# Seven block products for both halves of the up projection, and the first half's attention moved to other places

## The chip, the cores and the metric

The kernel runs on one core of one Trainium2 chip. The metric is the device time of one execution in microseconds (us). A time is the median of several runs; the profile is of one further execution, which has its own time.

Five engines work side by side, each with a queue of its own that it takes in order: TensorE (PE: matmuls, with PEld for the weight loads), VectorE (DVE), ScalarE (ACT), GpSimd (POOL), and SyncE (SP), which here issues nearly all transfers. An instruction may wait for others; whatever stands behind it in the same queue then waits too.

## The reference, cut to what matters

```python
SEQ, D_MODEL, D_FF = 2048, 1024, 2816        # 8 gMLP heads, 8 attention heads of 64
h = rms_norm(x, norm_mix_g); z = h @ w_in    # u, v, q, k, v_b, forget logits
out_a = spatial_gating(gelu(u), gelu(v), ...)           # per 128-position block
c = cumsum(log_sigmoid(f_logit))
out_b = softmax(q @ k.T / 8 + c[t] - c[s], s <= t) @ v_b # all 2048 positions, causal
x = x + concat(out_a, out_b) @ w_out
a = causal_conv3(rms_norm(x, norm_ffn_g) @ w_up) + b_conv  # 5632 channels
g, val = split(a)
x = x + (silu(g) * val) @ w_down
out = rms_norm(x, norm_final_g)
```

All inputs are float32. The kernel keeps float32's precision by splitting each operand of a large product into a high and a low part and computing three products (high·high, high·low, low·high).

## The kernel before

**Halves and blocks.** The 2048 positions are two halves of 1024, each of two blocks of 512, so there are four blocks tb = 0 to 3. `mm3` emits the three matmuls for each 128-deep slice of a product; a matmul of 128x512 is the unit of the work.

**Phase A** (`phase_a`, `a_half`) computes for each half keys and queries, values, and the gated heads; keys, queries, values and gated outputs go to DRAM tensors (`kx`, `qx`, `vd`, `mixh`, `mixl`). The first half goes in the order keys and queries, values, gated; the second half gated, values, keys and queries.

**Attention** is a Python generator, `b_stream`, over 32 pieces (8 heads for each tb). A piece has two parts, `b_max` and `b_mix`, and each yields 4·(tb+1) steps:
- a step of `b_max` has two matmuls into a PSUM tile `s`, a minimum over it on DVE (tile `part`) and an exponential with a sum on ACT (`s<-s,part`);
- a step of `b_mix` has two matmuls into `s`, an exponential on ACT (`e<-s`), a copy of its high part on ACT (`ph<-e`), the low part on DVE (`pl<-e,ph`), and two matmuls into `o`.

`s` has three buffers, `e` three, `ph` and `pl` two. Keys and values are read for 512 positions at a time (tiles `m` and `v`, two buffers each).

**What sets the order.** `mm3` calls `tick` after each matmul. `tick` adds 1 to a credit and runs one step of the stream when the credit reaches the rate:

```python
        if self.fill is not None:
            self.credit += 1
            while self.fill is not None and self.credit >= self.rate:
                self.credit -= self.rate
                self.step()
```

`need(tb)` emits steps until block tb is done. The code's order is not the final one: a scheduler that plans with a model of its own writes each engine's queue, and a step's instructions are given a priority 100 places ahead (`AHEAD_B`). So emitted steps may stand later in the queue than the code has them.

**After phase A.** `c_half(0)` multiplies the mixed heads of the first half with `w_out` and normalizes the rows. `d_half(0)` then does the first half's FFN: for each pair of channel groups (22 groups f of 128 gate and 128 value channels) `d_up` computes the up projection (24 matmuls for each of gate and value in each block, so 96 for a group), the convolution and the gate, and `d_down` multiplies the result at once with `w_down` (48 matmuls for a group), adding into `acc`. The attention stream runs on inside `c_half(0)` and `d_half(0)`, and its last pieces are taken by `need(3)` near `d_half`'s end.

**The second half.** `c_late` is `c_half` for the second half. `late_half` then computes the up projection by seven block products for each group f (`up_mms`, `prod`: P1 to P7, 12 matmuls each, so 84 instead of 96), from sums of weight blocks made by `up_sums` and sums of activations made once. `up_conv` does the convolution and the gate, and GpSimd's queue stores the result (`act_d[f]`). `down_half(1)` reads these back and multiplies with `w_down`, with eight PSUM banks `D`.

**Weights.** `load_unit` reads 512 KB into `raw` (two buffers), casts the high part on GpSimd (`whi<-raw`) and makes the low part on DVE (`wlo<-raw,whi`).

Of the kernel before, what the change touches and what calls it, by code (L numbers as in the profile page):

```python
# [31 lines left out]
RATES = [3.5, 4.0, 5.0, 4.6]  # L32
# [18 lines left out]
def f32(ap):  # L51
    return ap.bitcast(F32)


class Block:
# [44 lines left out]
    def need(self, tb):  # L100

        while self.done < 8 * (tb + 1):
            self.step()
# [76 lines left out]
    def constants(self):  # L180
# [19 lines left out]
        self.rows_d = t("rows", 8, [P, D])  # L200
# [36 lines left out]
    def phase_a(self):  # L237
        tc = self.tc
        with ExitStack() as es:
# [15 lines left out]
            def consts():  # L255
                with tc.issue_after(after):
                    self.a_consts(sp, pp)
                    self.b_consts()
# [4 lines left out]
            self.need(0)  # L263
            self.flush()

# [102 lines left out]
    def a_half(self, half):  # L368
# [28 lines left out]
        def keys_queries():  # L397
# [7 lines left out]
            groups = (("k", (2, 3)), ("q", (0, 1)), ("q", (2, 3))) if half == 0 else (("k", (2, 3)), ("q", (0, 1, 2, 3)))  # L405
            for kind, cs in groups:
                with self.tc.issue_after(self.rows_ins), self.tc.issue_after(self.pow_ins):
                    us = [(c, self.a_unit(kind, c)) for c in cs]
                for b in range(2):
                    for c, u in us:  # L410
                        channels(kind, c, *u, b)
                    if half == 1 and kind == "q" and b == 0:
                        self.need(0)
                        self.mix0 = self.load_mix(0)
# [16 lines left out]
        def gated():  # L431
# [5 lines left out]
            for t, ps in token_major(0):  # L437
                if t % 2 == 0:
                    self.a_mixed(vns[t // 2])
                self.a_gate(half * 2 + t // 4, t % 4, ps, vns[t // 2][:, t % 2, :])  # L440
                if half == 0 and t % 4 == 3:
# [131 lines left out]
    def b_consts(self):  # L573
        nc, bp = self.nc, self.bp
        ones = self.til(self.sp, [P, TB], F32, "st")[:2, :]
        nc.gpsimd.memset(ones, 1.0)
        for i in range(2):
            self.dma(self.ones_d[:, i * TB:(i + 1) * TB], ones)
        for k in self.kx:
            self.dma(k[:, 128:130, :], self.ones_d.unsqueeze(0).broadcast_to([8, 2, HALF]))  # L580
        self.mask = bp.tile([P, TB], BF16, name="mask")
# [5 lines left out]
        self.maskT = bp.tile([P, P], BF16, name="maskT")  # L587
# [4 lines left out]
        self.rowsel = bp.tile([8, 4, P], BF16, name="rowsel")  # L592
# [4 lines left out]
        self.M1 = [bp.tile([P, TB], F32R, name=f"m1_{j}") for j in range(2)]  # L597
        self.T1 = [bp.tile([P, TB], F32R, name=f"t1_{i}") for i in range(2)]
# [166 lines left out]
    def c_half(self, half, accp):  # L765
        nc, pp = self.nc, self.dpp
        w_out = self.a["w_out"][0].rearrange("(c p) n -> p c n", p=P)
        acc = []
        mix = [self.mix0, None]
        for b in range(2):  # L770
            mh, ml = mix[b]
            rows = []
            for t in range(4 * b, 4 * b + 4):
                x = self.til(accp, [P, D], F32, "acc")
                t0 = half * HALF + t * P
                self.dma(x, self.a["x"][0, t0:t0 + P, :])
                acc.append(x)
            for col in (b, 1 - b):
                if b == 0 and col == 1:
                    self.need(2 * half + 1)  # L780
                    mix[1] = self.load_mix(2 * half + 1)
                cs = slice(col * 512, (col + 1) * 512)
                if b == 0 or col == 0:
                    us = [self.load_unit(w_out[:, 2 * j:2 * j + 2, cs], 512) for j in range(4)]
                    wh = [us[k // 2][0][:, k % 2, :] for k in range(KC)]
                    wl = [us[k // 2][1][:, k % 2, :] for k in range(KC)]
                for t in range(4):
                    ts = slice(t * P, (t + 1) * P)
                    ps = self.til(pp, [P, TB], F32, "mm")
                    self.mm3(ps, [mh[:, k, ts] for k in range(KC)], [ml[:, k, ts] for k in range(KC)], wh, wl)  # L790
                    ac = acc[b * 4 + t]
                    nc.vector.tensor_tensor(ac[:, cs], ps, ac[:, cs], op=ALU.add)
                    if col == 1 - b:
                        row = self.til(self.dp, [P, D], F32, "ar")
                        r = self.row_scale(self.dp, ac, row)
                        nc.gpsimd.tensor_scalar(row, ac, r, 0.0, ALU.mult, ALU.add)
                        rows.append(row)
            hi, lo = self.hT[b] = self.parts(b)

            def turn(c, rows=rows, hi=hi, lo=lo):  # L800
                self.transpose_split(pp, "dn", [r[:, c * P:(c + 1) * P] for r in rows],
# [456 lines left out]
```

## Time and profile before

| what | value |
|---|---|
| median of 3 runs | 2564.45 us (2561.37 to 2567.49) |
| the profiled execution: its time, its span | 2568.74 us, 2567.0 us |
| PE busy | 2503.3 us, 98% of the span |
| VectorE busy | 1705.5 us, 66% |
| ScalarE busy | 1271.4 us, 50% |
| GpSimd busy | 302.6 us, 12% |
| granted TensorE clock, mean | 0.992 |
| transfers | 336.27 MB, 131 GB/s over the span |

The stages can be told by their tiles in the trace: phase A to about 640 us, `c_half(0)` and `d_half(0)` from there to 1776 us, `c_late` to about 1877 us, the seven products from 1878.5 to 2313 us, and `down_half(1)` from 2318.0 us to the end. Rows of groups give "busy us, mean ns of one | idle us of the engine before them, and what ended it". Rows of windows give the busy us of each engine in that stretch, the number of its instructions, the granted clock, the share of the transfer engines and GB/s.

### The profile page before, as it was taken

The page shows a single profiled execution, that of the slowest core. Times are in us where ns is not written, and L with a number is a line of the kernel's source. Part 1 is how long each engine was busy: PE and PEld are TensorE (multiplying, and loading weights), DVE is VectorE, ACT ScalarE, POOL GpSimd, SP SyncE. Part 2 cuts the span into 40 slices and gives each one's busy share as a digit, 9 for nine tenths or more (in the row PEclk, how much of TensorE's full clock was granted, in tenths as well). Part 3 has the DMA queues.
Part 4 walks back from the last instruction along what each step waited for, and adds up shares of the span by engine and source line. Part 5 has one row for each costly group of instructions (what it writes and reads, how often), then busy time and mean ns, then how long its engine had stood idle before and what let it go on. Part 6 is the DMA issues. An engine that isn't in the chain of part 4 may idle for free.

```text
span 2567.0 us, 32644 instructions
## 1 busy us (share of the span) xinstructions
PE 2503.3 (98%) x11346; PEld 2048.8 (80%) x11346; DVE 1705.5 (66%) x2997; ACT 1271.4 (50%) x2392; POOL 302.6 (12%) x336
## 2 busy tenths in 40 slices
PE   8999999999999999999999999999989999999998
PEld 6787777878788888888888888887868888887887
DVE  5237666555467777777777776766478888875443
ACT  4327777554356555455545544554245454544331
POOL 3204121000111011001100100111200000000000
PEclk9999999999999999999999999999999999999999
DMA  6863534666733333324323332347412222226461
GB/s 186 251 161 101 168 99 133 174 185 206 276 118 115 98 106 106 98 81 119 98 91 98 111 96 81 118 142 250 149 57 82 91 82 82 83 95 231 142 224 55
DMA packets 316032, 336.27 MB, mean 131 GB/s; under 512 B 49724, under 2 KB 218884, under 8 KB 315852
## 3 DMA queue, kind: packets, MB, share of 16 engines
q1 hardware_dynamic: 312700, 322.65, 41.6%
q0 software_dynamic: 3168, 11.54, 1.1%
q8 instruction: 90, 1.47, 0.2%
q14 instruction: 74, 0.61, 0.1%
HBM read 267.80 MB, written 66.46 MB: 130 GB/s over the span
## 4 chain that ended last, share of the span: by engine, by line
PE 86%; DMA 4%; DVE 4%; ACT 3%; issue 1%; POOL 1%; SPq 0%; POOLq 0%; DVEq 0%; ACTq 0%
PE mm L172 12%; PE mm L174 12%; PE mm L176 12%; PE D L1164 9%; PE dn L172 3%; PE dn L176 3%; PE dn L174 3%; PE A L1033 3%; PE A L1032 3%; PE A L1034 3%; PE s L656 2%; PE s L655 2%; PE s L717 2%; PE s L716 2%; PE o L705 2%; PE o L704 2%
## 5 line engine op out<-in xcount | busy, mean ns | idle before, releaser
L172 PE MATMUL mm<-thi,whi 128*128 128x512 f32 x960 | 376.9, 393 | 2.6 <-DVE vn L381 2.6
L174 PE MATMUL mm<-tlo,whi 128*128 128x512 f32 x960 | 377.3, 393 | 0.0
L176 PE MATMUL mm<-thi,wlo 128*128 128x512 f32 x960 | 376.9, 393 | 0.2 <-DVE wlo L126 0.2
L664 ACT ACTIVATE s<-s,part 128x512 f32<-128x512 f32 (+3 forms) x320 | 190.7, 596 | 214.7 <-DVE part L659 139.1
L728 DVE TENSOR_TENSOR pl<-e,ph 128x512 fp32r<-128x512 f32 (+1 forms) x320 | 203.5, 640 | 110.7 <-PE o L705 66.7
L172 PE MATMUL mm<-whi,thi 128*128 128x512 f32 x640 | 254.5, 400 | 8.0 <-POOL whi L114 6.3
L174 PE MATMUL mm<-wlo,thi 128*128 128x512 f32 x640 | 255.1, 399 | 3.1 <-DVE wlo L126 3.0
L176 PE MATMUL mm<-whi,tlo 128*128 128x512 f32 x640 | 253.1, 396 | 0.0
L722 ACT ACTIVATE e<-s 128x512 f32<-128x512 f32 (+1 forms) x320 | 166.9, 533 | 169.8 <-PE s L717 83.5
L727 ACT ACTIVATE ph<-e 128x512 fp32r<-128x512 f32 (+1 forms) x320 | 179.5, 568 | 132.3 <-PE o L704 118.6
L114 POOL TENSOR_SCALAR whi<-raw 128x1024 fp32r<-128x1024 f32 x130 | 148.2, 1142 | 801.7 <-PE mm L176 229.4
L172 PEld LDWEIGHTS mm<-thi,whi 128*128 128x128 f32 x960 | 180.8, 188 | 41.1 <-DVE vn L381 3.1
L174 PEld LDWEIGHTS mm<-tlo,whi 128*128 128x128 f32 x960 | 180.8, 188 | 37.9
L176 PEld LDWEIGHTS mm<-thi,wlo 128*128 128x128 f32 x960 | 180.9, 188 | 37.9 <-DVE wlo L126 0.7
L126 DVE TENSOR_TENSOR wlo<-raw,whi 128x1024 fp32r<-128x1024 f32 x130 | 163.1, 1257 | 59.4 <-POOL whi L114 59.2
L659 DVE TENSOR_REDUCE part<-s 128x1 f32<-128x512 f32 x192 | 128.0, 684 | 44.6 <-PE s L656 43.5
L850 DVE TENSOR_TENSOR acc<-dn,acc 128x512 f32<-128x512 f32 x176 | 120.9, 687 | 52.4 <-PE dn L176 51.2
L172 PEld LDWEIGHTS mm<-whi,thi 128*128 128x128 f32 x640 | 121.5, 190 | 33.9 <-POOL whi L114 7.8
L174 PEld LDWEIGHTS mm<-wlo,thi 128*128 128x128 f32 x640 | 121.8, 190 | 29.7 <-DVE wlo L126 6.6
L1164 PE MATMUL D<-dh,ah 128*128 128x512 f32 x352 | 138.3, 393 | 5.2 <-ACT ah L913 5.2
L176 PEld LDWEIGHTS mm<-whi,tlo 128*128 128x128 f32 x640 | 121.5, 190 | 24.1
L172 PE MATMUL dn<-whi,ar 128*128 128x512 f32 x352 | 138.2, 393 | 0.0
(299 smaller groups left out, 5525.6 us busy)
## 6 DMA issues: line engine op xcount, KB each, us to landing
m<-kx SPq DMA_DIRECT2D x160, 256.0 KB
raw<-in_w_up_dram SPq DMA_DIRECT2D x44, 512.0 KB
rawl<-in_w_up_dram SPq DMA_DIRECT2D x44, 512.0 KB
rawl<-in_w_down_dram SPq DMA_DIRECT2D x44, 512.0 KB
m<-kx SPq DMA_DIRECT2D x160, 136.0 KB
raw<-in_w_in_dram SPq DMA_DIRECT2D x40, 512.0 KB
v<-vd SPq DMA_DIRECT2D x80, 256.0 KB
x<-in_x_dram SPq DMA_DIRECT2D x24, 512.0 KB
```

The lines of the kernel that those rows point to most:

```text
L114: self.cast_ins = self.nc.gpsimd.tensor_scalar(out, in_, 1.0, 0.0, ALU.mult, ALU.add).ins
L126: nc.vector.tensor_tensor(lo, raw, f32(hi), op=ALU.subtract)
L172: mm(ps, lhsT=ah[k], rhs=bh[k], start=k == 0, stop=False)
L174: mm(ps, lhsT=ah[k], rhs=bl[k], start=False, stop=False)
L176: mm(ps, lhsT=al[k], rhs=bh[k], start=False, stop=k == n - 1)
L659: nc.vector.tensor_reduce(dst, ps, axis=AX.X, op=ALU.min)
L664: nc.scalar.activation(ps[:, :n], ps[:, :n], AF.Exp, scale=-1.0, bias=dst, accum_out=ls[:, tt, sb:sb + 1])
L722: nc.scalar.activation(e[:, c], ps[:, c], AF.Exp, scale=-1.0)
L727: nc.scalar.activation(ph[:, c], e[:, c], AF.Copy)
L728: nc.vector.tensor_tensor(pl[:, c], e[:, c], f32(ph[:, c]), op=ALU.subtract)
L850: nc.vector.tensor_tensor(ac, ps, ac, op=ALU.add)
L1164: nc.tensor.matmul(bank[t, col], lhsT=x[i][:, ts], rhs=w[j][:, cs], start=f == 0 and i + j == 0, stop=f == NF - 1 and i == 1)
```

## The change

The first half now takes the second half's path. `c_late` becomes `c_half(half)`, `late_half` becomes `up_half(half)`, and `d_up`, `d_down`, `d_half` and `d_out` go. The order of stages (`run`) is: phase A, `c_half(0)`, `up_half(0)`, `down_first`, `c_half(1)`, `up_half(1)`, `down_half(1)`.

- The first half's up projection has 22·84 matmuls instead of 22·96.
- Both halves of phase A go keys and queries, values, gated. Attention is cut in two lists: the first 20 pieces (tb 0, tb 1 and four heads of tb 2) run in phase A, which ends with `drain()`; the other 12 run in `down_first`, which ends with `drain()` too. `up_half(0)` has no attention.
- `up_conv` stores the first half's results in `act_d`, and the new `down_first` reads them and `w_down` back, 256-row units of 512 columns at a time, in each of two blocks (so `w_down` is read twice), with four PSUM banks `D0`. The rows before the FFN go through `rows_d`.
- The attention pools are closed after phase A and opened again before `down_first`, in the space that `up_half`'s activations and convolution tiles had.

```diff
-RATES = [3.5, 4.0, 5.0, 4.6]
+RATES = [3.7, 3.7, 2.6]
+EARLY = 4
...
+        keys_queries()
+        values()
         if half == 0:
-            keys_queries()
-            values()
-            self.start_fill(self.b_stream([(h, tb) for tb in range(4) for h in range(8)]), RATES[0])
-            gated()
+            pieces = [(h, tb) for tb in range(4) for h in range(8)]
+            self.pieces = pieces[:16 + EARLY], pieces[16 + EARLY:]
+            self.start_fill(self.b_stream(self.pieces[0]), RATES[0])
         else:
-            self.rate = RATES[1]
-            gated()
-            values()
-            keys_queries()
+            self.ready = True
+        gated()
+        self.rate = RATES[1]
...
+    def down_first(self):
...
+            def prep(n):
+                b, col, j = n // (NF), n // (NF // 2) % 2, n % (NF // 2)
+                cs = slice(col * 512, (col + 1) * 512)
+                w = self.load_unit(w_down[:, 2 * j:2 * j + 2, cs], 512)
+                xf = self.til(dp, [P, 2, TB], F32, "df2")
+                for i in range(2):
+                    self.dma(xf[:, i, :], self.act_d[2 * j + i][:, b * TB:(b + 1) * TB])
+                x = [self.til(dp, [P, 2, TB], F32R, "ah2"), self.til(dp, [P, 2, TB], F32R, "al2")]
+                self.both(x, xf)
+                parts.append((w, x))
+
+            prep(0)
+            self.bp_steps(6)
...
+                        for t in range(4):
+                            ts = slice(t * P, (t + 1) * P)
+                            for c in range(2):
+                                for i, k in ((0, 0), (0, 1), (1, 0)):
+                                    nc.tensor.matmul(banks[t], lhsT=x[i][:, c, ts], rhs=w[k][:, c, :],
+                                                     start=j + c + i + k == 0, stop=j == NF // 2 - 1 and c + i == 2)
+                                    self.tick()
...
+                    if (b, col) == (1, 0):
+                        self.need(2)
+                        self.mix0 = self.load_mix(2)
+            self.drain()
+            self.mix1 = self.load_mix(3)
...
+        self.phase_a()
+        for half in range(2):
+            self.accp = cstack.enter_context(tc.tile_pool(name="accp", bufs=1, reuse_waits="tile"))
+            if half:
+                self.down_first()
+            self.dpp = cstack.enter_context(tc.tile_pool(name="dps", bufs=1, space=PSUM, reuse_waits="tile"))
+            self.bstack.close()
+            self.open_half()
+            self.c_half(half)
+            cstack.close()
+            self.up_half(half)
+            self.ustack.close()
+            self.tqs.close()
+            if half == 0:
+                for i in range(2):
+                    self.up_conv(NF - 2 + i)
+                self.ystack.close()
+                cstack = self.c_open()
+                self.b_open()
+                self.b_consts()
+                self.start_fill(self.b_stream(self.pieces[1]), RATES[2])
+        self.down_half(1)
```

Counted over the whole built program, PE has 11019 instructions instead of 11283, DVE 2832 instead of 2998, ACT 2164 instead of 1965, GpSimd 299 instead of 338 and SP 1258 instead of 1130.

**The order on PE, last pieces of attention.** In the program before, the pieces of tb 3 stand among the matmuls of `d_half`. In these rows `mm` is the up projection, `dn` the down projection, `s` and `o` attention:

```order
L174 MATMUL dn_15580<-wlo_15528,ar_15445 128x512
L176 MATMUL dn_15580<-whi_15527,ar_15445 128x512
L172 MATMUL mm_15641<-thi_6872,whi_15603 128x512
L174 MATMUL mm_15641<-tlo_6873,whi_15603 128x512
L176 MATMUL mm_15641<-thi_6872,wlo_15604 128x512
L655 MATMUL s_13149<-m_1_491,t_1_493 128x512
L656 MATMUL s_13149<-m_3019_13117,t_3015_13110 128x512
L172 MATMUL mm_15641<-thi_6872,whi_15603 128x512
L655 MATMUL s_13161<-m_0_490,t_1_493 128x512
L705 MATMUL o_12780<-pl_13077,v_13016 128x128
```

In the changed program most pieces of tb 3 stand behind the matmuls of `down_first` and behind the first 216 matmuls of `c_half(1)`, with only their own kind around them:

```order
L714 MATMUL o_15153<-ph_15206,v_15157 128x512
L726 MATMUL s_15290<-t_1_2433_11425,m_1_2433_11423 128x512
L727 MATMUL s_15290<-t_3279_14494,m_3496_15285 128x512
L715 MATMUL o_15153<-pl_15207,v_15157 128x512
L714 MATMUL o_15153<-ph_15225,v_15216 128x512
L715 MATMUL o_15153<-pl_15226,v_15216 128x512
L714 MATMUL o_15153<-ph_15238,v_15216 128x512
L726 MATMUL s_15304<-t_1_2433_11425,m_1_2433_11423 128x512
L727 MATMUL s_15304<-t_3279_14494,m_3496_15285 128x512
L715 MATMUL o_15153<-pl_15239,v_15216 128x512
```

This stretch is rows 7040 to 7656 of PE's 10743: 595 matmuls of attention (541 when each is counted by its width of 512), 12 matmuls of `c_half(1)` and 22 small transposes and turns. It holds 80 steps of `b_max` and 110 of `b_mix`. In the program before, the longest run of attention matmuls without other work is 9 rows.

**The order on PE, end of phase A.** The last pieces before `c_half(0)` goes on. Here, too, the changed program has attention alone (rows 3120 to 3297, 174 matmuls, 151.5 by width, 15 steps of `b_max` and 36 of `b_mix`), where the program before goes on in the same place with phase A's own products:

```order
L172 MATMUL mm_6393<-whi_6180,thi_6022 128x512
L174 MATMUL mm_6393<-wlo_6181,thi_6022 128x512
L176 MATMUL mm_6393<-whi_6180,tlo_6023 128x512
L172 MATMUL mm_6393<-whi_6186,thi_6022 128x512
L716 MATMUL s_6365<-t_0_492,m_0_490 128x512
L716 MATMUL s_6379<-t_0_492,m_0_490 128x512
```

```order
L665 MATMUL s_6825<-m_0_79_498,t_0_79_500 128x512
L666 MATMUL s_6825<-m_1537_6785,t_1511_6660 128x512
L726 MATMUL s_6851<-t_1_79_501,m_1_79_499 128x512
L727 MATMUL s_6851<-t_1391_6199,m_1550_6846 128x512
L726 MATMUL s_6864<-t_1_79_501,m_1_79_499 128x512
L727 MATMUL s_6864<-t_1391_6199,m_1550_6846 128x512
```

The cover has moved: `c_half(0)`'s first block and part of its second now stand ahead of these rows.

**The order on SP, from `up_half(0)` to `down_first`.** In the changed program the first act rows that `down_first` reads (tile `df`, `df2` in the code) stand behind the loads of the reopened attention tiles:

```order
L74 DMA v_11741<-vd_78 128x4x128
L74 DMA v_11799<-vd_78 128x4x128
L74 DMA t_0_2433_11424<-ones_d 2x512
L74 DMA t_1_2433_11425<-ones_d 2x512
L74 DMA df_2437_11450<-act_104 128x512
L74 DMA df_2437_11450<-act_105 128x512
```

The tiles `t` lie where the convolution's tiles were, so these loads can go only when GpSimd's stores of the last `act_d` rows have landed. The program before had no such place: `d_half(0)` came straight behind `c_half(0)`, and `act_d` was read back only once, in `down_half(1)`.

More of the change, by code (lines that the diff above doesn't have):

```diff
@@ L102, in need, with drain @@
         while self.done < 8 * (tb + 1):
+            self.step()
+            self.count += 3
+            while self.late and self.late[0][0] <= self.count:
+                self.late.pop(0)[2]()
+    def drain(self):
+        while self.fill is not None:
             self.step()
@@ L199, in constants @@
         self.mixl = t("mixl", 4, [D, TB])
-        self.rows_d = t("rows", 8, [P, D])
+        self.rows_d = t("rows", 16, [P, D])
         self.act_d = t("act", NF, [P, HALF])
@@ L763, in load_mix @@
         return hi, lo
[L765 to L801, printed above, removed]
-                                     self.g_ffn[:, c:c + 1], hi[:, c, :], lo[:, c, :])
-            for c in range(KC):
-                self.defer(26 + 8 * c, lambda c=c, turn=turn: turn(c))
-        self.acc = acc
@@ L1131, in down_half, with bp_steps @@
+    def bp_steps(self, n):
+        for i in range(n):
+            self.step()
     def down_half(self, half):
```

212 lines of the change are left out of this document (77 added, 135 removed), and 2 rows, old and new, of the table BUFS.

## The prediction

> **What bounds the kernel now.** I read the busy totals first, then windows through the stages, then the waits of PE.
>
> ```profile
> PE 2503.3 (98%) x11346; PEld 2048.8 (80%) x11346; DVE 1705.5 (66%) x2997; ACT 1271.4 (50%) x2392; POOL 302.6 (12%) x336
> ```
>
> PE is idle for 64 us of 2567.0. The windows (busy us of PE, PEld, DVE, ACT, POOL; granted clock; share of the transfer engines; GB/s) show that this holds with attention in the mix and without:
>
> ```profile
> 340.00:420.00 80.00, 74.05 (x360) 59.23 (x358) 62.37 (x133) 60.42 (x108) 28.45 (x19) 1.00 0.34 102
> 560.00:640.00 80.00, 80.00 (x372) 65.89 (x371) 44.78 (x96) 38.79 (x89) 5.27 (x5) 1.00 0.68 201
> 640.00:720.00 80.00, 78.41 (x347) 64.06 (x346) 38.40 (x70) 27.88 (x66) 14.47 (x15) 0.98 0.75 256
> 1000.00:1200.00 200.00, 200.00 (x903) 165.31 (x902) 151.57 (x292) 103.91 (x221) 22.61 (x24) 1.00 0.35 103
> 1730.00:1780.00 50.00, 48.58 (x221) 39.76 (x219) 40.00 (x67) 28.36 (x53) 7.78 (x11) 1.00 0.81 254
> 1877.00:1900.00 23.00, 14.80 (x63) 10.38 (x61) 22.37 (x27) 11.49 (x13) 0.93 (x1) 0.91 0.25 69
> 2000.00:2100.00 100.00, 100.00 (x438) 81.84 (x437) 84.13 (x105) 52.19 (x80) 2.66 (x5) 1.00 0.25 81
> ```
>
> From 1000 to 1200 us (`d_half` with attention) PE never stops, and ACT is at 52%: attention's ACT work is hidden under matmuls of the FFN. From 2000 to 2100 us (seven products, no attention) PE never stops either, with DVE at 84%. So the time is PE's count of matmuls, as long as other PE work stands around attention. One place differs: from 1877 to 1900 us, where the second half goes from `c_late` to the products, PE is idle for 8.2 us.
>
> The rate of PE comes from the down projection, 1056 matmuls of one shape (first and last start):
>
> ```profile
> L1164 PE MATMUL D<-dh,ah x352: 389/389/794, 2318.0 to 2558.9; 128*128 128x512 f32 x176
> L1164 PE MATMUL D<-dh,al x352: 388/389/389, 2323.8 to 2559.3; 128*128 128x512 f32 x176
> ```
>
> (2559.3 - 2318.0)/1056 = 0.2285 us for each; the window at 2000 gives 0.2283.
>
> **What the change removes.** 22·12 = 264 matmuls of 128x512, all on the path: 264 · 0.2285 = **-60.3 us**. What ACT gains (199 instructions) and DVE exchanges in `up_half(0)` costs nothing: the window at 2000 us shows the same work at full PE. That cover has no attention in it, and neither has the new stage.
>
> **What it adds: attention without cover.** The two orders of PE are the point. Before, no more than 9 attention matmuls stand together. In the changed program 595 do before the second half of `c_half(1)`, and 174 at the end of phase A. There the time is that of the slowest engine of attention itself. Its instructions (mean ns of one behind the comma):
>
> ```profile
> L664 ACT ACTIVATE s<-s,part 128x512 f32<-128x512 f32 (+3 forms) x320 | 190.7, 596 | 214.7 <-DVE part L659 139.1 <-DVE part L661 60.7 <-DVE halo L823 5.3
> L664 ACT ACTIVATION_READ_ACCUMULATOR s<-s,part 128x1 f32 x320 | 63.0, 197 | 0.1
> L722 ACT ACTIVATE e<-s 128x512 f32<-128x512 f32 (+1 forms) x320 | 166.9, 533 | 169.8 <-PE s L717 83.5 <-DVE s L720 52.2 <-DVE pl L728 27.2
> L727 ACT ACTIVATE ph<-e 128x512 fp32r<-128x512 f32 (+1 forms) x320 | 179.5, 568 | 132.3 <-PE o L704 118.6 <-DVE pl L728 4.6 <-issue 3.1
> L739 ACT ACTIVATE op<-o 64x512 f32<-64x512 f32 x32 | 19.0, 594 | 32.1 <-PE o L705 31.7
> L659 DVE TENSOR_REDUCE part<-s 128x1 f32<-128x512 f32 x192 | 128.0, 684 | 44.6 <-PE s L656 43.5
> L728 DVE TENSOR_TENSOR pl<-e,ph 128x512 fp32r<-128x512 f32 (+1 forms) x320 | 203.5, 640 | 110.7 <-PE o L705 66.7 <-ACT ph L727 38.2 <-ACT a L820 2.4
> ```
>
> A step of `b_max` costs ACT 596 + 197 = 793 ns, DVE 684 and PE two matmuls (457); a step of `b_mix` costs ACT 533 + 568 = 1101 ns, DVE 640 and PE four (914). ACT is the slowest in both.
>
> Late stretch: 80 · 0.793 + 110 · 1.101 = 184.6 us, and the ends of seven pieces (`op` and, for each pair of heads, two more of about the same length, some 1.2 us a piece) 8.5: 193.1 us of ACT. PE has 541 matmuls by width, 541 · 0.2285 = 123.6 us, and that part was paid before too. So at least 69.5 us are new. The upper bound is ACT at the highest share that a window shows, 60.42/80 = 0.755: 193.1/0.755 = 256, 132 new. In that window PE was the bound, so the truth lies near the lower end: I take ACT's sum and 10% for waits between engines and for the loads of keys, 212.4, thus **+88.8 us**.
>
> End of phase A: 15 · 0.793 + 36 · 1.101 + 3 = 54.5 us of ACT against 151.5 · 0.2285 = 34.6 of PE: 19.9 at least, 72.2 - 34.6 = 37.6 at most; with 10%, **+25.4 us**.
>
> The other 4 pieces and the first of tb 3 stand among the 1056 `D0` matmuls and the 216 of `c_half(1)`, and their ACT work is hidden as now.
>
> **The seams.** From `up_half(0)` to `down_first`, PE's last product must first pass through the tail of the convolution, then the store, then SP's loads, since the reopened tiles lie where the convolution's were. The groups of that tail, in its order, with the split of a 512 KB tile on ACT (`dh<-rawl`) as the last:
>
> ```profile
> L1097 ACT ACTIVATE cv<-A 128x512 f32<-128x512 f32 x22 | 12.8, 581 | 0.4 <-PE A L1034 0.4
> L1120 ACT ACTIVATE ts<-cv,colB 128x1024 f32<-128x1024 f32 x44 | 54.7, 1244 | 28.4 <-DVE cv L1095 27.8
> L1121 DVE SCALAR_TENSOR_TENSOR ts<-cv,colA,ts 128x1024 f32<-128x1024 f32 x44 | 56.5, 1284 | 22.0 <-ACT ts L1120 21.8
> L1122 DVE SCALAR_TENSOR_TENSOR ts<-cv,colA,ts 128x1024 f32<-128x1024 f32 x44 | 56.4, 1282 | 0.8
> L1126 ACT ACTIVATE cv<-ts 128x1024 f32<-128x1024 f32 x22 | 23.4, 1061 | 6.9 <-DVE ts L1122 6.7
> L1127 DVE SCALAR_TENSOR_TENSOR ts<-cv,ts 128x1024 f32<-128x1024 f32 x22 | 26.8, 1218 | 1.2 <-ACT cv L1126 1.2
> L1128 DVE TENSOR_TENSOR ts<-ts 128x1024 f32<-128x1024 f32 x22 | 26.8, 1219 | 0.1
> L913 ACT ACTIVATE dh<-rawl 128x1024 fp32r<-128x1024 f32 x44 | 45.9, 1048 | 7.8 <-DMA rawl<-in_w_down_dram 6.0 <-PE D L1164 1.7
> ```
>
> The stores of `act` (issue in ns, then us to landing), and two loads of attention's tiles as they stand in the chain that ended last (start, us):
>
> ```profile
> L1129 POOL DMA_DIRECT2D act<-ts x22: 531/533/767, 1933.9 to 2331.6; - x22
> DMA to landing us min/median/max: 2.9/2.9/5.5
> ```
>
> ```profile
> 304.17 3.66 DMA m<-kx
> 315.85 4.60 DMA t<-qx
> ```
>
> The tail is 7.9 us, issue and landing of the store 3.4, a load 3.7 to 4.6 (256 KB, as `m` and `t`), GpSimd's clearing of the tiles some 0.5, and the split of the first rows 1.05: about 17 us. Behind such a gap PE starts slowly:
>
> ```profile
> 1779.86 0.40 PE L176 MATMUL mm<-whi,tlo 128*128 128x512 f32 x1
> 1784.44 1.22 PE L172 MATMUL mm<-whi,thi 128*128 128x512 f32 x2 [4.19 <-POOL whi L114]
> 1787.15 0.63 PE L174 MATMUL mm<-wlo,thi 128*128 128x512 f32 x1
> 1787.57 0.63 PE L176 MATMUL mm<-whi,tlo 128*128 128x512 f32 x1
> 1793.02 0.39 PE L174 MATMUL mm<-wlo,thi 128*128 128x512 f32 x1
> 1793.24 0.39 PE L176 MATMUL mm<-whi,tlo 128*128 128x512 f32 x1
> ```
>
> After 4.19 us of idling matmuls stand 0.42 us apart instead of 0.23, for some 5.6 us: 3 us lost. The seam is **+20 us**; 8 (the tail alone) to 27.
>
> From `c_half(0)` to `up_half(0)` the first half now has the seam that the second has at 1877 us: 8.2 us idle and 2 for the clock, **+10** (0, if fewer things are late, to 14).
>
> Behind the late stretch, the second block of `c_half(1)` needs the last heads: four end operations on ACT and DVE (some 3.3 us), store 2.9, load 4.2, clock 3: +14. In its place the 4.19 us wait and its slow clock (7) go, since `w_out` can be loaded during the stretch: **+7** (0 to 14).
>
> **Transfers in `down_first`.** Its rows on SP, from its first weight load to its last, move 81.8 MB (23.6 of `w_down`, 23.1 of act rows, the rest attention's and the rows'), while PE's 1056 + 254 matmuls take 299 us: 274 GB/s. Nothing before asks for that for so long; the windows at 640 and 1730 us show 256 and 254 GB/s with PE at 98 and 97%. At 256 it takes 320 us, +21; with no stall 0; at the 201 GB/s of 560 us, where PE did not ask for more, +108. I take **+10**, halfway between no stall and 256 GB/s.
>
> **Sum.** -60.3 + 88.8 + 25.4 + 20 + 10 + 7 + 10 = +100.9 us. Against the profiled execution that is 2568.74 + 100.9 = 2669.6; the median is 4.3 us below that execution, so 2564.45 + 100.9 = **2665 us**.
>
> **Rivals.**
>
> 1. *The clock falls in the uncovered stretches.* PE is busy there for only some 58%. If the granted clock halved (0.427 us for each matmul, as between 1784 and 1790 us), PE would be the bound: 541 · 0.427 = 231 us and 151.5 · 0.427 = 65, new 107 + 30 instead of 114: 2688 us. Against it: the window at 340 us has PE idle for 6 us in pieces with the clock at 1.00. The Trainium skill, "TensorE: Matmul & The Clock Gate", section "A second HAM failure mode: psum-queue depth-cycling", says that frequent short idling between groups of matmuls makes the clock gate swing between half and full rate; by it this rival would be the forecast, but the rows so far show the loss only behind a gap of 4 us. Chance 0.08.
> 2. *`down_first` starves.* SP's queue is in order, `raw` and `df2` have two buffers each, and weight loads stand among loads that wait for attention's buffers. Then it runs at the 201 GB/s above, +108 instead of +10: 2763 us. For it: 274 GB/s is asked. Against: PE is at 97% at 254 GB/s. Chance 0.10.
> 3. *ACT does not bound the stretches,* since `b_max` of one piece overlaps `b_mix` of another and the engines run at PE's pace. Then 114 us go: 2551 us, faster. With my other terms it decides when the two stretches lose under 13 us; ACT's instructions alone make it 89. Chance 0.05.
>
> **How the numbers follow.** The forecast has 0.74, the rivals 0.08, 0.10 and 0.05; 0.03 is left for a part of the third that ends near no change. The lower ends of the terms give -60.3 + 69.5 + 19.9 + 8 = +37, 2602 us. The upper ends of the stretches and seams give -60.3 + 132 + 37.6 + 27 + 14 + 14 + 10 = +174, 2739 us. The range 2602 to 2740 holds the forecast and rival 1 and leaves out 2 and 3. About 0.2% (5 us) can be told from no change: faster 0.05, same 0.03, slower 0.92.
>
> **What the new profile would show.** ACT at over 85% and PE near 60% in one stretch of about 210 us, ahead of the last 150 `mm` matmuls of `c_half(1)`, and in one of about 60 us after phase A; PE's waits there on `s`, `ph` and `pl`. An idle PE of some 17 us before the first `D0`. `up_half(0)` with PE full, in some 430 us. The forecast is wrong if ACT in the late stretch stays under 150 us, if PE waits on DMA or `wlo` for tens of us among the `D0` matmuls, or if the clock there is well below 1.

## The result: 2713 us, slower by 5.8%

| | median | runs |
|---|---|---|
| before | 2565.95 us | 2561.37 to 2567.49, 4 runs |
| changed | 2713.12 us | 2708.90 to 2717.81, 4 runs |

The ratio is 1.0577, 95% interval 1.0552 to 1.0602: +147 us, where +101 was forecast (2665, range 2602 to 2740). The spans of the two profiled executions differ by 141.8 us (2708.8 against 2567.0); the readings below are made against that.

The page of the changed kernel, totals and the granted clock in 40 slices:

```profile
PE 2528.3 (93%) x11082; PEld 2012.9 (74%) x11082; DVE 1780.3 (66%) x2831; ACT 1400.2 (52%) x2593; POOL 263.1 (10%) x297
PEclk9999999999989999999699999987999999999999
```

PE has 264 instructions fewer and is busy 25 us longer, and idle for 180 us instead of 64. So part of the loss is idle time and part is matmuls that run slowly; the clock's row shows three dips. Windows of the changed kernel at these places, with the same columns as before (busy us of PE, PEld, DVE, ACT, POOL; granted clock; transfer share; GB/s):

```profile
750.00:818.00 68.00, 51.38 (x188) 33.06 (x187) 42.14 (x98) 54.14 (x123) 2.21 (x4) 0.85 0.38 118
818.00:880.00 62.00, 57.27 (x268) 45.76 (x267) 41.84 (x57) 24.70 (x31) 9.33 (x8) 0.97 0.41 136
880.00:1300.00 420.00, 413.36 (x1788) 337.20 (x1788) 352.48 (x427) 215.32 (x342) 12.69 (x23) 0.99 0.24 77
1300.00:1346.00 46.00, 2.98 (x8) 1.83 (x7) 13.50 (x12) 4.05 (x5) 9.51 (x17) 0.53 0.95 333
1346.00:1670.00 324.00, 321.77 (x1425) 263.50 (x1425) 217.54 (x337) 163.32 (x332) 49.81 (x48) 0.99 0.66 214
1740.00:1960.00 220.00, 188.40 (x639) 120.57 (x638) 143.23 (x293) 172.41 (x401) 0.00 (x0) 0.85 0.45 137
```

They are: the end of phase A (attention alone up to 809.8 us, then a wait), the end of `c_half(0)`, `up_half(0)`, the seam, `down_first`, and the late stretch of attention alone. `up_half(0)` and `down_first` run with PE full, as forecast; the two attention stretches and the seam carry the loss. Four waits of PE, from the end of phase A, the seam and the late stretch:

```profile
PE dn L157 <- ACT acc L833: 8.0, 1, 8.0
PE s L665 <- DMA t<-ones_d: 43.0, 1, 43.0
PE mm L182 <- DMA thi<-mixh: 8.9, 1, 8.9
PE s L665 <- ACT s L674: 9.3, 14, 1.5
```

The first is `c_half(0)`'s: its rows were stored by 738 us, but their normalization stands behind attention in ACT's queue and starts at 812.4.

### The profile page after: what moved, and what is told of

It reads as the page before. It is cut to its first block, busy times and chain, and to the rows that moved or that the text cites. A ratio compares the mean times of both kernels' runs of the same rounds, so it can differ in the third digit from the quotient of the medians.

```text
span 2708.8 us, 32673 instructions
## 1 busy us (share of the span) xinstructions
PE 2528.3 (93%) x11082; PEld 2012.9 (74%) x11082; DVE 1780.3 (66%) x2831; ACT 1400.2 (52%) x2593; POOL 263.1 (10%) x297
## 4 chain that ended last, share of the span: by engine, by line
PE 74%; DMA 6%; DVE 4%; ACT 4%; issue 2%; POOL 0%; SPq 0%; DVEq 0%; POOLq 0%; ACTq 0%
PE D L1054 9%; PE D L1111 9%; PE A L910 6%; PE A L911 6%; PE A L912 6%; PE mm L182 5%; PE mm L186 5%; PE mm L184 4%; PE B L911 3%; PE B L912 3%; PE B L910 3%; PE s L665 2%; PE s L726 2%; PE s L666 2%; DMA m<-kx 2%; PE s L727 2%
## 5 line engine op out<-in xcount | busy, mean ns | idle before, releaser
L124 POOL TENSOR_SCALAR whi<-raw 128x1024 fp32r<-128x1024 f32 x108 | 130.0, 1205 | 750.0 <-PE D L1054 215.4
L665 PE MATMUL s<-m,t 96*128 96x512 f32 (+2 forms) x320 | 132.5, 434 | 70.6 <-DMA t<-ones_d 43.0
L796 DVE TENSOR_TENSOR al<-df,ah 128x1024 fp32r<-128x1024 f32 (+1 forms) x88 | 87.4, 996 | 124.4 <-ACT ah L795 123.5
L795 ACT ACTIVATE ah<-df 128x1024 fp32r<-128x1024 f32 (+1 forms) x88 | 74.1, 845 | 181.1 <-PE D L1111 101.4
L136 DVE TENSOR_TENSOR wlo<-raw,whi 128x1024 fp32r<-128x1024 f32 x108 | 133.3, 1234 | 44.0 <-POOL whi L124 43.7
L665 PEld LDWEIGHTS s<-m,t 96*128 96x128 f32 x320 | 65.8, 210 | 110.2 <-ACT s L674 45.2
L1000 DVE SCALAR_TENSOR_TENSOR ts<-cv,colA,ts 128x1024 f32<-128x1024 f32 x88 | 113.8, 1293 | 48.4 <-ACT ts L999 47.7
L726 PE MATMUL s<-t,m 128*128 128x512 f32 (+1 forms) x320 | 126.7, 397 | 15.1 <-ACT s L674 8.0
L1054 PE MATMUL D<-whi,ah 128*128 128x512 f32 x352 | 139.7, 397 | 0.3 <-ACT ah L795 0.3
L1054 PE MATMUL D<-wlo,ah 128*128 128x512 f32 x352 | 138.8, 394 | 0.0
```

The costliest lines, as they stand in the source:

```text
L665: nc.tensor.matmul(ps[:, :n], lhsT=t1[0:96, ts], rhs=m1[0:96, :n], start=True, stop=False)
L726: nc.tensor.matmul(ps[:, c], lhsT=m1[:, ks], rhs=t1[:, c], start=True, stop=False)
L1054: nc.tensor.matmul(banks[t], lhsT=x[i][:, c, ts], rhs=w[k][:, c, :], start=j + c + i + k == 0, stop=j == NF // 2 - 1 and c + i == 2)
```

## The experiments

Each time stands beside runs of the kernel before on the same chip (medians 2568 to 2569); ratios are to those.

### Is it attention at all? (e5, e6)

Both kernels were run without attention. In the diff for the changed kernel (the same for the kernel before), the stream emits no piece, and attention's rows of `mixh`/`mixl` are zeroed once:

```diff
+        for m in self.mixh + self.mixl:
+            for r in range(512, 1024, P):
+                self.dma(m[r:r + P, :], tf)
...
         for h, tb in pieces:
+            self.done += 1
+            yield
+        return
```

> The kernel before without its attention: no piece is computed, and the attention rows of mixh/mixl are zeros. Attention is 377 us of PE at full clock (95 + 282 in the windows), so if it costs there only its matmuls, the time is about 2190 us (2170 to 2220).

> The changed kernel without its attention, in the same way. T1 (nearly all of the loss is attention that stands without enough other work): what stays of the change is -60 us of matmuls and the two seams, some 30 to 45 and 5 to 18 us, so this kernel is within -30 to +10 us of e5's, where with attention the difference is +147. Rival (the new stage and its transfers cost it, attention or not): 60 us or more above e5's.

Measured: 2148.72 us (2145.38 to 2150.26) for e5, 2151.44 us (2149.91 to 2152.30) for e6: +2.7 us. (e5 is 21 us below the range expected: attention holds PE busy for 416 us in the kernel before, 2503.3 less 2087.7 without it, not for 377.) The new stage and the seven products together cost nothing net: PE is busy 50.7 us less in e6's profile than in e5's and idle 56.0 more, since the seam is there without attention too. The wait in e6:

```profile
PE D L1063 <- ACT ah L804: 45.9, 3, 43.9
```

So 144 of the 147 us are there only when attention is.

### The seam (e1, e8)

In the changed kernel SP's in-order queue issues this while PE idles (start, issue us):

```profile
1297.43 4.82 SPq L74 DMA_DIRECT2D acc<-rows  x6
...
1312.62 2.63 SPq L74 DMA_DIRECT2D tlo<-mixl  x1
...
1326.61 4.37 SPq L74 DMA_DIRECT2D m<-kx  x4
...
1338.49 2.40 SPq L74 DMA_DIRECT2D t<-ones_d  x2
1341.12 0.82 SPq L74 DMA_DIRECT2D df<-act  x2
```

The last store of `act` had been issued at 1311.82. The rows of `acc` and the mixed heads, which nobody needs yet, stand ahead of what PE waits for. e1 holds them behind the first `df` loads:

```diff
-                                self.dma(rows[t], self.rows_d[4 * b + t])
+                                with tc.issue_after(self.dfi):
+                                    self.dma(rows[t], self.rows_d[4 * b + t])
...
-            self.mix1 = self.load_mix(3)
+            with tc.issue_after(self.dfi):
+                self.mix1 = self.load_mix(3)
```

> Changed kernel, but on SP's queue the reads of rows into acc and of the last two blocks of mixh/mixl stand behind the first reads of act rows (df), instead of ahead of them. T1 (SP's in-order queue makes the seam): PE's idle time between up_half(0) and the first attention matmul falls from 43.0 us to the 17 of the tail's chain (15 to 24), and the time by 20 to 27 us against the changed kernel, to about 2690. Rival (the tail of the convolution and the reopened tiles make the seam, or the transfers as such, wherever they stand): idle stays at 35 or more, the time within 8 us of 2713.

Measured: 2718.49 us (ratio 1.0581, 1.0557 to 1.0605), no faster. The idle time fell only from 43.0 to 33.8 us, since a second chain lay right behind the first one. Its links in e1 (GpSimd and SP, start and us):

```profile
1314.02 0.58 POOL L1008 DMA_DIRECT2D act<-ts  x1 [3.64 <-DVE ts L1007]
1318.13 0.52 POOL L592 MEMSET mask<- 128x512 bf16 x1 [3.53 <-DMA act<-ts]
...
1322.81 0.98 POOL L611 MEMSET m<- 8x512 f32 x2
...
1327.73 1.97 SPq L74 DMA_DIRECT2D t<-ones_d  x2
1329.89 0.82 SPq L74 DMA_DIRECT2D df<-act  x2
```

The last product starts at 1299.19, so the tail up to the store takes 14.8 us, not the 7.9 of the forecast. Then the store lands, GpSimd clears the reopened tiles for some 6 us, the rows of ones are loaded, and then the act rows. The 9 us gained were lost in the late stretch, 234 us there instead of 220 (it begins with 12 more rows of attention in PE's order). e8 shortens that second chain:

```diff
-            nc.gpsimd.memset(f32(m[64:128, :]), 0.0)
-            nc.gpsimd.memset(f32(m[96:104, :]), 1.0)
+            nc.vector.memset(f32(m[64:128, :]), 0.0)
+            nc.vector.memset(f32(m[96:104, :]), 1.0)
         for t in self.T1:
-            nc.gpsimd.memset(f32(t[64:128, :]), 0.0)
-            self.dma(f32(t[66:68, :]), self.ones_d[:, 0:TB])
+            nc.vector.memset(f32(t[64:128, :]), 1.0)
```

> e1_seam, with the constants of the reopened attention tiles written by VectorE instead of GpSimd, and the rows of ones in t written in the same memset instead of by two transfers. If the seam is a chain (tail 14 us, store 4, memsets 6, ones 4, act rows 4), PE's idle time there goes from 33.8 to 22 to 27 us and the time 7 to 12 us below e1's. If the act rows would come no sooner, it stays at 31 or more.

Measured: 2711.43 us (1.0565, 1.0542 to 1.0588). The median is 7 us below e1's, but the runs overlap. The wait is 28.9 us, above the 22 to 27 expected, and hangs on another load, `t<-cc`, that stands behind six loads of `raw`. A chain cut at one link hung on the next. What removes most of it is e10, below: other work for PE in the meantime.

### What bounds attention that stands alone (e2, e3)

e2 takes a copy of the late pieces away from ACT:

```diff
-            nc.scalar.activation(ph[:, c], e[:, c], AF.Copy)
+            if self.second:
+                nc.gpsimd.tensor_scalar(ph[:, c], e[:, c], 1.0, 0.0, ALU.mult, ALU.add)
+            else:
+                nc.scalar.activation(ph[:, c], e[:, c], AF.Copy)
```

> Changed kernel, but for the 12 late pieces the copy ph<-e is made on GpSimd instead of ACT; the order on PE is nearly the same. T1 (ACT's instructions bound the uncovered stretch): ACT's work in it falls from 172 us to about 112, VectorE's 143 is then the largest, and the stretch falls from 220 us to 165 to 190, the time by 30 to 55 us. T2 (the stretch is bound by waits within one piece, by the chain s to e to ph to pl to o, which a slower copy on GpSimd lengthens): the stretch stays at 210 to 240 and the time within 15 us of 2713. T3 (the halved clock makes PE the bound): the stretch stays near 220 with the clock still near 0.85.

Measured: 2718.64 us (1.0588, 1.0573 to 1.0604). The window of the stretch, from the last product ahead of it (1741.9) to PE's last `o` (1966.6):

```profile
1742.00:1967.00 225.00, 194.00 (x642) 122.87 (x640) 155.14 (x293) 125.37 (x290) 81.45 (x112) 0.85 0.46 134
```

ACT's work fell from 172 to 125 us and the stretch stayed, at 225 us against 220. So my sum of ACT's instructions, though it gave nearly the right number, did not name what holds the stretch up. (GpSimd's copies took 0.73 us each, ACT's 0.60, so a step's own chain grew longer; that alone leaves ACT under suspicion until e9 and e12.) e3 asks about the clock: it keeps PE busier with one more matmul in each step of `b_max`.

```diff
                 ps = self.til(pp, [P, TB], F32, "s")
+                if tb == 3:
+                    nc.tensor.matmul(ps[:, :n], lhsT=t1[0:96, ts], rhs=m1[0:96, :n], start=True, stop=True)
```

> Changed kernel with one matmul more (96 rows deep, its result overwritten by the next) in each step of b_max of the last block of positions: 128 more, about 80 of them in the late uncovered stretch, 18 us of PE at full clock. T1 (ACT and the waits of the pieces bound the stretch): it stays at 215 to 228 us, and the 48 others cost 0.23 us each where PE is full: the time is 5 to 15 us above 2713. T3 (the fall of the clock costs the time, since PE has too little to do): the clock there rises from 0.85 to 0.93 or more and the stretch falls to 195 to 212 us. If PE itself bounds, the stretch becomes 235 or more.

Measured: 2732.29 us (1.0637, 1.0622 to 1.0653).

```profile
1760.00:1982.00 222.00, 185.82 (x696) 123.47 (x695) 138.80 (x286) 165.68 (x388) 0.00 (x0) 0.94 0.46 132
```

The clock rose from 0.85 to 0.94. The stretch holds 80 added matmuls (57 more in all, since some steps of `b_mix` now stand ahead of it), and PE was busy no longer than before (185.8 against 188.4 us). But the stretch took 222 us, not the 195 to 212 expected if the clock alone set its time, and PE's idle time went from 32 to 36. What the clock gave, the added matmuls used up, so this run can't tell what the slow clock costs. (The 48 added matmuls where PE is full are some 11 of the 19 us that e3 lost in all.)

The changed kernel's own trace says more. These are sums over its late stretch: first seven pieces between 1760 and 1924 us in which the granted clock was 0.50, then the rest, at 1.00:

```profile
sum 64.83, PE 60.78 PEld 36.80 DVE 41.94 ACT 43.95 POOL 0.00; mean PE 8.68 PEld 5.26 DVE 5.99 ACT 6.28 POOL 0.00
sum 154.81, PE 126.16 PEld 82.94 DVE 101.12 ACT 127.14 POOL 0.00; mean PE 15.77 PEld 10.37 DVE 12.64 ACT 15.89 POOL 0.00
```

At half clock PE is busy 94% of the time and ACT 68%; at full clock it is 81 and 82%. Had ACT gone on at 82%, its 44.0 us would have taken 53.5 instead of 64.8. So the slow clock costs the stretch some 11 us, an estimate from these rows.

### Cover without buffers (e4), and with them (e7)

e4 forces attention to keep up with `D0`, so that nothing is left for the late stretch:

```diff
-                                    nc.tensor.matmul(banks[t], lhsT=x[i][:, c, ts], rhs=w[k][:, c, :],
+                                    with tc.issue_after(self.att[-10]):
+                                        nc.tensor.matmul(banks[t], lhsT=x[i][:, c, ts], rhs=w[k][:, c, :],
```

> The order of e1_seam, and each matmul of D0 is placed on PE behind the second s matmul of attention issued ten before it in the code, so attention keeps up with D0: no uncovered run of attention is left behind down_first. T1 (attention without cover costs what PE's work could have hidden): the late stretch of 220 us disappears, down_first with attention takes 445 to 480 us up to the first matmuls of c_half(1) instead of about 544 with the stretch, and the time falls by 85 to 115 us beside e1_seam's 20 to 27: about 2590 (2573 to 2625). Rival (the attention steps cannot keep pace with D0's matmuls, or the transfers of down_first starve beside them, wherever they are put): the time falls by less than 50 us beyond e1_seam's.

Measured: 2704.47 us (1.0521, 1.0498 to 1.0544): 14 us below e1, where 85 to 115 were expected. The late stretch is gone, but `down_first` takes 573 us:

```profile
1343.00:1916.00 573.00, 517.25 (x2121) 396.69 (x2120) 377.32 (x669) 358.87 (x785) 52.46 (x49) 0.95 0.63 197
```

At the rate of the window 1346 to 1670 above (1425 matmuls in 324 us), 2121 would take 482. So "without cover" was not the whole cause either. The waits in that window, of PE and then of SP's queue (us in total, times, longest):

```profile
PE s L667 <- ACT s L676: 13.7, 19, 1.8
PE s L668 <- DMA t<-qx: 8.0, 8, 2.3
PE s L728 <- DMA m<-kx: 7.6, 7, 3.1
PE s L667 <- DMA t<-qx: 7.2, 6, 2.0
```

```profile
SPq L76 <- PE s L729: 103.9, 35, 6.6
SPq L76 <- PE s L668: 96.8, 37, 8.4
```

PE waits for queries and keys, and SP's queue waits for PE's last matmul on the old ones. On PE `b_max` of one piece and `b_mix` of the piece before stand one behind the other, 12 or 16 steps each. A piece's queries (`t`) are read in its `b_max` and once more in its `b_mix`, after the next piece's `b_max`. So both buffers of `t` are held until the last `s` of a `b_mix`, and the queries that the very next step needs can only be loaded then:

```profile
1512.50 0.28 PE L729 MATMUL s<-t,m 128*128 128x128 f32 x1
1512.70 0.45 SPq L76 DMA_DIRECT2D t<-qx  x1
```

All of PE's waits for `t` stand in the first two steps of a `b_max`. Of the keys, with two buffers of each kind, one block of four steps can be loaded ahead. A step of attention has some 3 matmuls of `D0` beside it here; before it had 4.6 to 5 of the FFN, and from 1000 to 1200 us PE never stopped with the same two buffers. Each such wait costs more than itself:

```profile
1516.85 0.47 PE L667 MATMUL s<-m,t 96*128 96x512 f32 x1 [1.17 <-DMA t<-qx]
...
1519.47 0.63 PE L1058 MATMUL D<-wlo,ah 128*128 128x512 f32 x1
1519.89 0.63 PE L1058 MATMUL D<-whi,al 128*128 128x512 f32 x1
1520.32 0.63 PE L1058 MATMUL D<-whi,ah 128*128 128x512 f32 x1
1520.75 0.46 PE L1058 MATMUL D<-wlo,ah 128*128 128x512 f32 x1
1521.05 0.40 PE L1058 MATMUL D<-whi,al 128*128 128x512 f32 x1
```

Behind waits of 0.56 us (at 1514.7) and 1.17 us the matmuls stand 0.43 us apart, and 0.23 again from 1521 us on.

e7 gives attention more buffers there. The space is `thi`/`tlo` of the second block, 32 KB of each partition, which is now opened only after `down_first`:

```diff
+                BUFS.update(dict(m1=5, m2=5, v=4, t1=3, t2=3, e=4, ph=3, pl=3))
...
-        self.tpool = [es.enter_context(...) for b in range(2)]
+        self.tpool = [es.enter_context(...) for b in range(1 if self.second else 2)]
...
                 self.down_first()
+                self.tpool.append(cstack.enter_context(tc.tile_pool(name="tpool1", bufs=1, reuse_waits="tile")))
```

> e4_hold10 with more buffers for attention in down_first, in the 32 KB that the second block's thi/tlo leave unused until then: keys m five of each kind instead of two, v four, t three, e, ph and pl one more. T1' (attention spread over D0 stays slow because a piece's keys and queries can be loaded only when the last matmul has left their two buffers, 58 us of waits for loads, each with a slow clock behind it): down_first goes from 573 us to 480 to 520, the waits on m, t and v fall under 15 us, and the time is 50 to 95 us below e4's 2704. Rival T2' (the ring of three s tiles, PE to VectorE to ACT, sets the pace): waits for loads go, but those on ACT's s grow, and the time is within 25 us of e4's. T3' (bandwidth): the same with loads still late.

Measured: 2639.33 us (1.0274, 1.0258 to 1.0290), 65 us below e4. (The 58 us of waits in that text counted PE's weight loads beside its matmuls; PE's own are some 32.)

```profile
1341.00:1853.00 512.00, 483.30 (x2133) 384.92 (x2134) 380.76 (x676) 360.02 (x792) 51.20 (x49) 0.99 0.68 209
```

Nearly the same work in 512 us, the clock at 0.99. Of the 61 us gained, 27 are idle time (55.8 to 28.7) and 34 are matmuls that run at full rate. The transfers run at 209 GB/s instead of 197, so bandwidth was not the limit. The wait for the first load of `t`, 33.1 us, is now PE's only one for a load around that window.

### The late stretch with buffers alone (e9, e12)

e9 has the same buffers but no matmul held, so PE has nearly the order of the changed kernel (`D0` starts ahead of attention). Against e1:

```diff
+                BUFS.update(dict(m1=5, m2=5, v=4, t1=3, t2=3, e=4, ph=3, pl=3))
...
                 self.down_first()
+                self.tpool.append(cstack.enter_context(tc.tile_pool(name="tpool1", bufs=1, reuse_waits="tile")))
```

> e1_seam with the buffers of e7_hold10_buffers, but no matmul held: the order on PE is that of the changed kernel, with its uncovered stretch. It tells what bounds attention that stands alone. If it is the two buffers of keys and queries (loads that cannot start early), the stretch goes from 220 us to 165 to 190 and the time 30 to 55 us below e1's 2718. If it is the ring of three s tiles and ACT's work in turn, it stays at 200 or more, and the time within 20 us of e1's.

Measured: 2660.13 us (1.0356, 1.0335 to 1.0376), 58 below e1 (30 to 55 expected). The late stretch, from the last product ahead of it to the last `o`:

```profile
1723.00:1909.00 186.00, 165.14 (x638) 107.80 (x636) 140.25 (x292) 165.46 (x399) 0.00 (x0) 0.97 0.51 150
```

Nearly the same instructions as in the changed kernel's 220 us (638 matmuls against 639, ACT 399 against 401), now in 186: PE busy 165 instead of 188, idle 21 instead of 32, clock 0.97. So 23 of the 34 us are matmuls that run faster and 11 are idle time. ACT is at 89%, and PE's 165 us are as much: with loads that come in time the stretch comes near the bound that the prediction had from the start, but that ACT alone sets it isn't shown. Beside e1, whose stretch took 234 us, the rest of the gain is ahead of it: `D0` begins earlier, and the seam's wait is 10.3 us.

e12 adds the buffers of keys, values and queries, but not those of `e`, `ph` and `pl`:

```diff
-                BUFS.update(dict(m1=5, m2=5, v=4, t1=3, t2=3, e=4, ph=3, pl=3))
+                BUFS.update(dict(m1=5, m2=5, v=4, t1=3, t2=3))
```

> e9_buffers with the added buffers of keys, values and queries alone (m five of each kind, v four, t three); e, ph and pl as in the changed kernel. If late loads are what the two buffers cost, the time is within 10 us of e9's 2660 and the uncovered stretch 175 to 190 us. If the ring from e over ph and pl to o was the bound, it stays above 205 us and the time above 2685.

Measured: 2664.79 us (1.0366, 1.0349 to 1.0383), within 5 us of e9.

```profile
1715.00:1918.00 203.00, 182.06 (x664) 118.43 (x662) 149.95 (x316) 179.08 (x428) 0.00 (x0) 0.91 0.51 145
```

This stretch holds 664 matmuls, 0.306 us each, against 0.344 in the changed kernel and 0.292 in e9. So it missed the 175 to 190 us, but its verdict on time came in: the buffers of loads, with the earlier `D0` that came with them, carry 53 of the 58 us. Keys, values and queries were not parted.

### Work for PE in the seam, and phase A (e10, e11)

e10 is e7 with the first 144 matmuls of `D0`, whose act rows were stored long before, ahead of attention. It also sets attention's last rate from 2.6 to 2.4:

```diff
-RATES = [3.7, 3.7, 2.6]
+RATES = [3.7, 3.7, 2.4]
...
-            self.bp_steps(6)
...
+                                    if self.nd == 144:
+                                        self.gate = last.ins
+                                        d, r, k2 = self.dfs[2]
+                                        with tc.issue_after(d), tc.issue_after(r), tc.issue_after(k2):
+                                            self.b_consts()
+                                            self.bp_steps(6)
...
+                    if self.gate:
+                        gs.enter_context(self.tc.issue_after(self.gate))
```

> e7_hold10_buffers, with the first 144 matmuls of D0 ahead of attention on PE, and on SP and GpSimd the loads and memsets of attention behind those of D0's first six units. D0's first units need nothing of the last act rows, so if the seam is the wait of attention's tiles for the convolution's space, PE's 33.1 us of idling there becomes 5 to 12, and the time falls by 15 to 28 us below e7's 2639, to 2611 to 2624; a few us go back since attention has fewer matmuls around it. If it stays above 2635, the seam is D0's own.

Measured: 2616.09 us (1.0193, 1.0169 to 1.0217), 23 below e7. All waits of PE from 1280 to 1360 us are now:

```profile
PE D L1064 <- ACT ah L803: 11.2, 2, 8.1
PE D L1064 <- DVE al L804: 1.3, 1, 1.3
```

So 12.5 us of the gap are left. The 8.1 us end at 1354, behind the 144 matmuls: SP issues the next act rows (1346.02) only behind attention's first loads.

e11 spreads attention in phase A too, with a hold like e4's around the products of `mm3`:

```diff
+                with self.tc.issue_after(self.att[-8]):
+                    mm(ps, lhsT=a, rhs=b, **kw)
```

> e10_d0_first, with each product's matmul of phase A placed on PE behind the second s matmul of attention issued eight before it, so that no run of attention is left at the end of phase A. If attention without cover costs there what it costs in the late stretch, the 27 to 32 us of excess go, less what attention loses with its two buffers of keys in phase A (as e4 against e7): 5 to 30 us below e10's, 2585 to 2615. If it is no faster than e10, two buffers hold attention up in phase A whatever stands beside it. The kernel before, at 2569, is not reached in either case.

Measured: 2629.96 us (1.0251, 1.0228 to 1.0275), 14 above e10, where 5 to 30 below were expected; `up_half(0)`'s first product starts 11 us later than in e10. As in e4, cover with two buffers does not pay; more of them weren't tried in phase A. PE's largest waits there, from 300 to 850 us:

```profile
PE s L677 <- ACT s L686: 11.7, 8, 3.2
PE s L677 <- DMA t<-qx: 9.6, 5, 5.6
```

In e10 these were 8.7 and 1.8 us. The 8.0 us behind attention, which e10 still has, are gone in e11.

No version beats the kernel before; e10 is the nearest, 97 us below the changed kernel and 48 above the kernel before.

## Why the prediction was right, and which terms were off

By terms of the sum, predicted and measured (us):

| term | predicted | measured |
|---|---|---|
| 264 matmuls fewer | -60.3 | fits e6 - e5, not measured alone |
| late stretch | +88.8 | 219.8 - 2.7 (12 products) - 123.6 = +93.5 |
| end of phase A | +25.4 | 59.5 (750.3 to 809.8) - 34.6 = +24.9, and +8.0 of wait behind it |
| seam to `down_first` | +20 | 46 less 1.8 for its 8 matmuls = +44 |
| seam to `up_half(0)` | +10 | 4.7 + 6.6 idle = +11 |
| last heads to `c_half(1)` | +7 | 8.9 of wait and a slow clock behind it, less the old 7: some +5 |
| transfers in `down_first` | +10 | 0: PE 321.8 of 324 us |

These sum to 126, of the 142 between the spans. The other 16 lie mostly in the first 750 us: counting each matmul by its width at 0.2285 us, the changed kernel takes 94 us more than that up to 750 us, the kernel before 80 up to 640. Since e6 against e5 leaves only 2.7 us, they come with attention; that they are its denser packing into phase A was only argued.

- **Direction and size.** Attention without cover was the largest part of the loss, and its price came out within 6% in both stretches; that was partly luck, as said below. The 8.0 us behind phase A's stretch had no term: the sum took `c_half(0)`'s normalization as free, and it stood behind attention on ACT.
- **The mis-sized term is the seam**, 20 predicted (8 to 27), 44 measured. The step that failed is the working of tail (7.9), store, load and clearing of the tiles (some 0.5). I had read in the order on SP that `df` stands behind attention's loads, but took no account of the rows and mixed heads that the queue would issue ahead of these. The tail took 12.1 us (from the last product at 1299.73 to the store at 1311.82), with two `wlo` of `w_down` among its steps on VectorE. And clearing took some 6 us, not 0.5, with the rows of ones to be loaded behind it.
- **ACT as the bound of the stretches** was nearly the right number for a wrong reason, and so luck. ACT was at 78%, not over 85%; e2 took 47 us from ACT and changed nothing. The sum itself was too large: ACT's instructions in the late stretch add up to 199 us (193 forecast), but they overlap and keep ACT busy for 171. What filled the gap up to 220 were the late loads of two buffers each (e9, e12) and the slow clock behind them.
- **Rival 1, the clock,** was half seen. Two windows of the stretch:

```profile
1760.00:1780.00 20.00, 18.62 (x43) 10.85 (x44) 13.66 (x31) 14.92 (x40) 0.00 (x0) 0.57 0.37 119
1780.00:1790.00 10.00, 9.86 (x42) 6.83 (x40) 6.65 (x12) 10.00 (x21) 0.00 (x0) 1.00 0.51 154
```

The clock swings between about half and full. The Trainium skill, "TensorE: Matmul & The Clock Gate", section "A second HAM failure mode: psum-queue depth-cycling", says so of frequent short idling, and the trace agrees (0.57 and 1.00). But it was at half for 65 of 220 us, not throughout, and by the estimate above that cost some 11 us. In e3 the clock rose to 0.94 and the stretch was no shorter, but with 80 matmuls more in it. How much the slow clock adds to each late load, here and among `D0` in e4, was not parted from the wait itself by a run: buffers removed both.
- **Rival 2, starving transfers,** is refuted: PE was full in `down_first` at 214 GB/s. I had also counted 254 attention matmuls in that stage; it holds 369, or 316 by width, so the 274 GB/s were not asked for.
- **Rival 3** would have needed attention at PE's pace; e9 came nearest, still 186 us against 124.

## What to carry to other kernels

Work with a long chain through several engines is free only while other work stands around it at a density that its buffers can bear; before such work is packed closer, count who holds each load buffer at the time the next load should go: queries that are needed again one pass later hold both of two buffers and leave none to load ahead. An engine's summed work gives an estimate, not a cause: take work from it (e2), or let its inputs come earlier (e9, e12). Adding work to an engine to speed up its clock (e3) spends what the clock gives, and so tells little. And at a border between two stages, what helped most was to put other ready work into the gap (e10), not to cut the chain link by link (e1, e8).

## What was new about the hardware here

- In e4, behind waits of 0.56 and 1.17 us, PE ran at about half rate for some 3 us (0.43 instead of 0.23 us a matmul; granted clock 0.50 from 1517.5 to 1520.9); the prediction had seen that only behind 4.19 us.
- Where attention stands alone, a slow clock changes which engine is the busiest: in the changed kernel's late stretch PE was busy 94% and ACT 68% at half clock, 81 and 82% at full clock.
